# A fused transformer pair on one core: the first expert pair's rows summed from h, other weight slots, larger last pieces

## The chip, the cores and the metric

The program runs on one core of one Trainium2 chip. The metric is device time in microseconds (us) of one execution; smaller is better. The core has five engines with a queue each: PE (TensorE: matrix products and transposes), DVE (VectorE), ACT (ScalarE), POOL (GpSimd) and SP (SyncE, which here only starts transfers). Each engine takes its own instructions in the order in which they were laid down; semaphores tie the engines together. Transfers run on 16 DMA engines.

## What is computed

Two layers over 512 tokens of width 1024 in fp32. The first has a state-space and attention mixer and then a mixture of 64 experts; the second has a neighbourhood attention and a gated linear attention and then a dense feed-forward. The change lies in the experts:

```python
g_sel = argmax(t @ w_router_group)             # one of 8 groups for each token
top_logit, top_local = top_k(in_group, 2)      # two of its 8 experts
gate = softmax(top_logit) * p_group
# the tokens are sorted by expert into blocks; for each block:
hid = silu(xb @ w_gate[e]) * (xb @ w_up[e])    # 1024 -> 512
y_buf = hid @ w_down[e]                        # 512 -> 1024
y = zeros_like(t).at[tok_sorted].add(y_buf * gate)
```

Every expert has 6 MB of weights (gate, up and down, 2 MB each), and all 64 are read once.

## The kernel before, in words

**Experts in pairs.** Each expert gets 64 slots for tokens (more go through a loop that is entered only when one has more), so two experts fill the 128 rows of a product. `experts` (L973) walks over 32 pairs, i = 0 to 31. For a pair it multiplies the 128 gathered token rows (`xg`, turned so that the width lies on the partitions) by the gate and the up weights, 32 instructions for each (16 products with 64 output rows, in two instructions each), makes `hid`, turns it, multiplies by the down weights (32 instructions more), splits the result into a high and a low part and adds it back to the tokens of h with a 0/1 matrix (`combine`, L1162).

**The router.** The last output product of the mixer (`wout_tail`, L385) gives h in four tiles c of 128 tokens. As each is added up (L405), `route_tile` (L793) turns it, multiplies it by the router weights (L807) and writes the rows to `hd` in DRAM. `choose` (L863) finds the two experts and, by a product with a triangle of ones (L909, L910), the place of each token among its expert's; the result is `keys`. `gather_first` (L944) makes of the keys a 0/1 matrix `S0` for the first 256 slots (four experts, two pairs).

**The rows of a pair.** From pair 2 on the rows are fetched from `hd` by an indirect DMA on POOL's queue (`fetch`, L850) into one of four `rows` tiles, and turned by `gained` (L1021): eight PE transposes, and two DVE instructions that multiply by the norm's gain. For the first two pairs there is no fetch: `route_tile` splits h into a high part `hnH` (ACT, L812) and a low part `hnL` (POOL, L813), and `gather_first` multiplies both by `S0`, 16 matmuls of 256 columns for each token tile c, 64 in all, straight into the turned form; eight DVE instructions at L1042 bring it to `xg`.

**The weight slots.** Weights go through eight slots of 2 MB, used in turn (`ring`, L113), in the order G, U, D (gate, up, down) of each pair, two tiles each. Slots 0 to 2 lie in `ringp`, 3 and 4 in `ring2`, 5 in `ring3`, and 6 and 7 are the tiles tagged A1 and A2 (`w16x` in the profile). A1 and A2 hold the mixer's normed input first, and then `hnH` and `hnL`. So pair 0 fills slots 0 to 5, and the gate weights of pair 1 go to A1 and A2. All weights are started by SP in program order, so a tile that waits for its slot holds back all behind it. At most eight of SP's transfers are under way at a time; a tile goes in two pieces of 1 MB (four in the first six pairs, eight for pair 1's gate weights, L987).

**The last pair.** `pair` (L134) loads pair 31 in smaller pieces, the two experts' in turn, five for each tile. Behind it SP starts the second layer's first weights (L1729). The second layer's first transposes (`begin.turn`) lie among this pair's products.

**Order.** Instructions of an engine are laid down by a planner that may move them where nothing depends on it; the products of the expert loop are pinned to program order (L1000).

Of the kernel before, what the change touches and what calls it, by code (L numbers as in the profile page):

```python
# [6 lines left out]
FT = mybir.dt.float32  # L7
FR = mybir.dt.float32r
# [3 lines left out]
OP = mybir.AluOpType  # L12
# [3 lines left out]
P = 128  # L16
T = 512
D = 1024
KT = 8
NT = 4  # L20
# [8 lines left out]
class Net:  # L29
# [83 lines left out]
    def ring(self, shape, dma, parts=1):  # L113

        self.nring = getattr(self, "nring", -1) + 1
        n = [p.bufs for p in self.rings]
        m = self.nslots = sum(n) + (0 if self.held is None else 2)
        k = self.nring % m
        t = (self.held or {}).get(k)
        if t is None:  # L120
            if k >= sum(n):
                t = self.per.tile([P, 4096], FT, name="w16x", tag=("A1", "A2")[k - sum(n)])
            else:
                x = k
                for p, b in zip(self.rings, n):
                    if x < b:
                        break
                    x -= b
                t = p.tile([P, 4096], FT, name="w16", tag="w16")
            if self.held is not None:  # L130
                self.held[k] = t
        return self.load(t, shape, dma, parts)

    def pair(self, shape, dmas):  # L134

        tiles = [self.ring(shape, d, 0) for d in dmas]
        n, m = shape[1:]
        quarter = n // 4
        cuts = [(j, j + quarter, 0, m) for j in range(0, n - quarter, quarter)]
        cuts += [(n - 2, n - 1, 0, m), (n - 1, n, 0, m)] if n == 8 else [(n - 1, n, 0, m // 2), (n - 1, n, m // 2, m)]  # L140
        for a, b, c, d in cuts:
            for t, w in zip(tiles, dmas):
                self.nc.sync.dma_start(t[:, a:b, c:d], w[:, a:b, c:d])
        return tiles

    def load(self, t, shape, dma, parts=1):
# [610 lines left out]

    def route_start(self, keep, pool):
        nc, per = self.nc, self.per
        self.hn = (per.tile([P, NT, D], FR, name="hnH", tag="A1"), per.tile([P, NT, D], FR, name="hnL", tag="A2"))  # L760
        self.rpool = pool

        it = self.it = keep.tile([P, 512], FT, name="it")
        nc.gpsimd.iota(it.rearrange("p (e s) -> p e s", e=8), pattern=[[512, 8], [1, 64]], base=0,
                       channel_multiplier=0, allow_small_or_imprecise_dtypes=True)
        sk = self.sk = keep.tile([P, 32], FT, name="sk")
        for s in range(2):
            nc.gpsimd.iota(sk[64 * s:64 * s + 64, :], pattern=[[1024, 32]], base=512 * s, channel_multiplier=1,
                           allow_small_or_imprecise_dtypes=True)
        w64 = self.w64 = pool.tile([P, 64], FT, name="w64", bufs=1)  # L770
        nc.gpsimd.iota(w64, pattern=[[-1, 64]], base=64, channel_multiplier=0, allow_small_or_imprecise_dtypes=True)

# [12 lines left out]
        self.parts10 = keep.tile([P, NT, 5, 2], FR, name="parts10")  # L785

        self.hd = self.dram.tile([T, D], FT, name="hd")
        self.tops = keep.tile([P, 3, NT], FT, name="tops")
        self.S0 = keep.tile([P, NT, 256], FR, name="S0")
        self.keys = keep.tile([P, 2, NT], FT, name="keys")  # L790
        self.pl = self.psum("y")

    def route_tile(self, c):  # L793

        nc, V, h, pool, hn = self.nc, self.nc.vector, self.H, self.rpool, self.hn
        pl = self.pl[:, c * 72:(c + 1) * 72]
        xTs, turned = [], []
        for q in range(2):
            xT = pool.tile([P, 4, P], FT, name="xT", bufs=4)
            p = self.psum("sc")  # L800
# [8 lines left out]
                    self.order(t, m)  # L809
        V.tensor_copy(self.lg[:, c, :], pl)  # L810
        nc.scalar.dma_start(self.hd[c * P:(c + 1) * P, :], h[:, c, :])
        nc.scalar.copy(hn[0][:, c, :], h[:, c, :])  # L812
        nc.gpsimd.tensor_tensor(hn[1][:, c, :], h[:, c, :], hn[0][:, c, :].bitcast(FT), OP.subtract)  # L813
        sq = pool.tile([P, D], BF, name="sq", tag="xT", bufs=4)
        nc.scalar.activation(sq, h[:, c, :], AF.Square, accum_out=self.ss4[:, c:c + 1])

# [122 lines left out]
        self.nc.scalar.copy(self.counts, p[:, :64])  # L939

    def gather_start(self):
        self.first = [self.psum(t) for t in ("pj", "pj", "tp", "tp")]

    def gather_first(self, c):  # L944

        nc, V = self.nc, self.nc.vector
# [1 line left out]
        V.tensor_scalar(eq, self.it[:, :256], self.keys[:, 0, c:c + 1], None, op0=OP.is_equal)  # L948
        V.scalar_tensor_tensor(self.S0[:, c, :], self.it[:, :256], self.keys[:, 1, c:c + 1], eq, op0=OP.is_equal,
                               op1=OP.add)  # L950
        for j in range(KT):
            for part in range(2):
                nc.tensor.matmul(self.first[j // 2][:, (j % 2) * 256:(j % 2 + 1) * 256], self.hn[part][:, c, j::8],
                                 self.S0[:, c, :], start=c + part + j % 2 == 0, stop=j % 2 == 1 and c == 3 and part == 1)

    def route(self, keep, tail):

# [15 lines left out]
    def experts(self, keep, pool, front, inner, then):  # L973
        nc, i = self.nc, self.ins
# [15 lines left out]
        ahead = None  # L990

        self.rows = [front.tile([P, D], FT, name=f"rows{n}", bufs=1) for n in range(4)]
        for r in self.rows:
            nc.gpsimd.memset(r, 0.0)


# [16 lines left out]
        def values(q):  # L1013

            rs, gs, tok, at = self.slots(front, self.S0, [sk[:, 2 * q + x:2 * q + x + 1] for x in range(2)], 2)
            if q:
                for x in range(2):
                    self.fetch(self.rows[2 * (q % 2) + x], tok[:, x:x + 1])
            vals[q] = rs, gs, at

# [13 lines left out]
            yield  # L1034


        Xs, vals = {}, {}
        for x in range(2):
            Xs[x] = front.tile([P, KT, P], FT, name="xg", bufs=2)
        for x in range(2):  # L1040
            for n in range(4):
                V.tensor_tensor(Xs[x][:, 2 * n:2 * n + 2, :],  # L1042
                                self.first[n].rearrange("p (j s) -> p j s", j=2)[:, :, x * P:x * P + P],
                                self.g8[:, 2 * n:2 * n + 2].unsqueeze(2).to_broadcast([P, 2, P]), OP.mult)
        self.factors(front)
        self.gate(front)
        self.warm(AF.Silu, self.vals[:, 0, 2:3])
# [5 lines left out]
            for _ in range(min(n, len(todo))):  # L1053
                self.combine(*todo.pop(0), pin=True)

        evict = []
        for i in range(32):
            q, pr = i // 2, i % 2
            e0 = 2 * i
# [39 lines left out]
            next(turn, None)  # L1099
            bring(4)  # L1100
            next(turn, None)
            for e in evict:
                e()
            evict.clear()
            if pr == 0 and 0 < q < 15:
                values(q + 1)

# [2 lines left out]
            if not last:  # L1110
# [8 lines left out]
                    todo.extend((ST, yH, yL, t, hs) for t in range(NT))  # L1119
                if i == 0:  # L1120
                    values(1)
            else:
                ys = [self.psum(t) for t in ("y", "pj")]
                for j in range(4):
# [679 lines left out]
```

## Time and profile before

| | |
|---|---|
| runs | 2073.59, 2072.85, 2068.12 us; median 2072.85 us |
| profiled execution | 2071.55 us, of it the span of the core 2069.8 us |
| busy PE, DVE, ACT, POOL | 1954.0 (94%), 962.6 (47%), 537.4 (26%), 204.6 (10%) us |
| HBM read | 500.15 MB, 245 GB/s over the span; 415 to 426 GB/s from about 466 to 1294 us |
| chain that ended last | DMA 46%, PE 43%, DVE 6% |

A row of a timeline is: start, length in us, engine, line, operation, out<-in, shapes, count; in square brackets the idle time of the engine before it and what ended that. PE's busy time is modelled and counts overlapping matmuls once. The granted clock of PE is given as a share of full speed: 1.00 is 2.4 GHz, 0.50 is 1.2 GHz.

### The profile page before, as it was taken

The numbers are of one execution on the slowest core, as the hardware profiler recorded it, in microseconds if no ns is written. First come the engines' busy times: TensorE is split into PE (matmuls) and PEld (weight loads), VectorE is DVE, ScalarE is ACT, GpSimd is POOL, SyncE is SP. The second block draws the span as 40 slices with busy tenths as digits, with TensorE's granted clock in tenths as the row PEclk, the third lists the DMA queues.
The fourth block names the chain that finished last, engine by engine and source line by source line (L and its number), as shares of the span: only waits on it lengthen the run. The fifth ranks groups of instructions, "written<-read, shape, count | busy, mean of one in ns | idle before, by whom it ended". The sixth has DMA issues, their size and how long they took to land.

```text
span 2069.8 us, 24164 instructions
## 1 busy us (share of the span) xinstructions
PE 1954.0 (94%) x9551; PEld 1227.6 (59%) x9551; DVE 962.6 (47%) x1899; ACT 537.4 (26%) x902; POOL 204.6 (10%) x252
## 2 busy tenths in 40 slices
PE   7999999999999999999999999998999999999998
PEld 6788777744443344344334334346777778888886
DVE  5774667743532343243243333334564664344345
ACT  5773545311000100000010000024352423232232
POOL 5111324210000000000000000002111100000000
PEclk9999999999999999999999999999999899999999
DMA  7312112579999999999999999983212112223221
GB/s 201 111 42 82 58 66 82 201 290 416 415 424 424 423 425 425 424 423 426 424 424 423 422 423 424 393 314 67 90 41 82 42 41 92 83 81 122 84 80 41
DMA packets 116939, 494.04 MB, mean 239 GB/s; under 512 B 16658, under 2 KB 23257, under 8 KB 78424
## 3 DMA queue, kind: packets, MB, share of 16 engines
q1 hardware_dynamic: 110024, 483.64, 58.5%
q0 software_dynamic: 6208, 6.74, 1.5%
q10 hardware_dynamic: 592, 2.10, 0.3%
q8 instruction: 76, 1.25, 0.2%
q14 instruction: 39, 0.32, 0.0%
HBM read 500.15 MB, written 6.15 MB: 245 GB/s over the span
## 4 chain that ended last, share of the span: by engine, by line
DMA 46%; PE 43%; DVE 6%; ACT 2%; issue 2%; SPq 1%; POOL 0%; DVEq 0%; ACTq 0%; POOLq 0%
DMA w<-in_w_up 8%; DMA w<-in_w_down 8%; PE pj L185 7%; PE pj L184 7%; DMA w<-in_w_gate 7%; PE pj L186 7%; DMA w16x<-in_w_up 7%; DMA w16x<-in_w_gate 7%; DMA w16x<-in_w_down 7%; PE sc L185 3%; PE sc L184 3%; PE sc L186 3%; DMA w<-in_w_in 1%; DVE M L703 1%; PE y L185 1%
## 5 line engine op out<-in xcount | busy, mean ns | idle before, releaser
L1001 PE MATMUL pj<-w,xg 128*64 128x512 f32 x1536 | 370.0, 609 | 36.1 <-DMA w<-in_w_up 35.0
L1001 PEld LDWEIGHTS pj<-w,xg 128*64 128x64 f32 x1536 | 121.2, 140 | 273.9 <-issue 213.4
L165 DVE TENSOR_TENSOR wL<-w,wH 128x1024 fp32r<-128x1024 f32 x135 | 168.4, 1248 | 203.5 <-ACT wH L164 202.7
L1088 DVE SCALAR_TENSOR_TENSOR hid<-pj,slots,hid 128x512 f32<-128x512 f32 x32 | 24.0, 751 | 464.3 <-PE pj L1001 464.3
L164 ACT CAST wH<-w 128x1024 fp32r<-128x1024 f32 x136 | 142.3, 1048 | 340.3 <-PE pj L185 166.9
L1169 DVE TENSOR_TENSOR H<-sc,H 128x512 f32<-128x512 f32 x256 | 161.5, 682 | 9.5 <-PE sc L1166 7.1
L1001 PE MATMUL pj<-w16x,xg 128*64 128x512 f32 x512 | 126.1, 615 | 17.1 <-DMA w16x<-in_w_up 15.0
L1166 PE MATMUL sc<-yH,ST 128*128 128x512 f32 x256 | 113.2, 442 | 0.6 <-DVE H L1169 0.6
L1097 ACT COPY hT<-tp 128x512 f32<-128x512 f32 x32 | 18.8, 587 | 352.1 <-PE tp L1095 352.1
L852 POOL DMA_INDIRECT rows<-hd,tok x30 | 30.3, 1009 | 806.5 <-issue 646.7
L186 PE MATMUL pj<-n3H,wL 128*128 128x512 f32 (+1 forms) x272 | 103.6, 381 | 0.8 <-DVE wL L165 0.8
L184 PE MATMUL pj<-n3H,wH 128*128 128x512 f32 (+1 forms) x272 | 103.6, 381 | 0.0
L185 PE MATMUL pj<-n3L,wH 128*128 128x512 f32 (+1 forms) x272 | 103.5, 381 | 0.0
L184 PE MATMUL pj<-A,wH 128*128 128x512 f32 x240 | 97.8, 408 | 4.0 <-ACT wH L164 2.8
L1166 PE MATMUL sc<-yL,ST 128*128 128x512 f32 x256 | 101.1, 395 | 0.0
L185 PE MATMUL sc<-wL,mixH 128*128 128x512 f32 x252 | 98.5, 391 | 0.0
L184 PE MATMUL sc<-wH,mixH 128*128 128x512 f32 x252 | 98.5, 391 | 0.0
L186 PE MATMUL sc<-wH,mixL 128*128 128x512 f32 x252 | 98.2, 390 | 0.0
L1001 PEld LDWEIGHTS pj<-w16x,xg 128*64 128x64 f32 x512 | 39.6, 141 | 98.7 <-issue 72.4
L185 PE MATMUL pj<-A,wH 128*128 128x512 f32 x240 | 97.7, 407 | 0.0
L186 PE MATMUL pj<-A,wL 128*128 128x512 f32 x240 | 96.9, 404 | 0.5 <-DVE wL L165 0.5
L1001 PE MATMUL y<-w,hT 128*64 128x512 f32 x384 | 89.4, 608 | 0.7 <-ACT hT L1097 0.7
(579 smaller groups left out, 3382.5 us busy)
## 6 DMA issues: line engine op xcount, KB each, us to landing
w<-in_w_gate SPq DMA_DIRECT2D x76, 1024.0 KB, 19.6
w<-in_w_down SPq DMA_DIRECT2D x76, 1024.0 KB, 19.6
w<-in_w_up SPq DMA_DIRECT2D x72, 1024.0 KB, 20.9
w<-in_w_ff SPq DMA_DIRECT2D x16, 2048.0 KB, 7.9
w16x<-in_w_up SPq DMA_DIRECT2D x28, 1024.0 KB, 19.7
w<-in_w_in SPq DMA_DIRECT2D x12, 2048.0 KB, 10.9
w16x<-in_w_down SPq DMA_DIRECT2D x24, 1024.0 KB, 20.5
w16x<-in_w_gate SPq DMA_DIRECT2D x24, 1024.0 KB, 20.4
```

What stands on the lines that cost most here:

```text
L164: a = nc.scalar.copy(H, src)
L165: b = (engine or nc.vector).tensor_tensor(L, src, H.bitcast(FT), OP.subtract)
L184: m = mm(out, lH, rH, start=first, stop=False)
L185: mm(out, lH, rL, start=False, stop=False)
L186: mm(out, lL, rH, start=False, stop=last)
L703: nc.vector.tensor_tensor(t, t, cb[g], OP.mult)
L852: self.nc.gpsimd.indirect_dma_start(out=rows, out_offset=None, in_=self.hd[:, :], in_offset=bass.IndirectOffsetOnAxis(ap=tok, axis=0), bou ...
L1001: return self.pin(nc.tensor.matmul(*a, **k))
L1088: V.scalar_tensor_tensor(hid, pu, r, hid, op0=OP.mult, op1=OP.mult)
L1097: nc.scalar.copy(hT.rearrange("p j s -> p (j s)"), p)
L1166: m = nc.tensor.matmul(p, ST[:n, t * P:(t + 1) * P], y[:n], start=k == 0, stop=k == 1)
L1169: nc.vector.tensor_tensor(h[:, t, hs], p, h[:, t, hs], OP.add)
```

## The change

Four things change.

- `hnH` and `hnL` and the instructions that make them are gone. `gather_first` makes `S0` as before, and then sums only the 128 slots of pair 0, in plain order: for each token tile two fp32 products of 512 columns with `S0` as the stationary side and h itself as the moving side, into two banks of PSUM. Behind the router one bank is copied to `rows[0]` by DVE and the other by ACT, and `gained(0)` turns them as for any later pair.
- Pair 1's rows are fetched like all later ones: `values(0)` starts one fetch, and `gained(1)` stands behind the down products of pair 0, with its two DVE instructions right behind.
- The slots' order is: `ringp`, `ringp`, `ring2`, `ring2`, A1, A2, `ringp`, `ring3`. A1 and A2 hold pair 0's down weights; pair 1's gate weights go to the third slot of `ringp` and to `ring3`.
- The last pair is loaded in two pieces for a gate or up tile, and three for a down tile (a half and two quarters).

```diff
@@ ring
-            if k >= sum(n):
-                t = self.per.tile([P, 4096], FT, name="w16x", tag=("A1", "A2")[k - sum(n)])
+            p = self.rings[0 if self.held is None else (0, 0, 1, 1, 0, 0, 0, 2)[k]]
+            if self.held is not None and k in (4, 5):
+                t = self.per.tile([P, 4096], FT, name="w16x", tag=("A1", "A2")[k - 4])
             else:
...
@@ pair
-        cuts = [(j, j + quarter, 0, m) for j in range(0, n - quarter, quarter)]
-        cuts += [(n - 2, n - 1, 0, m), (n - 1, n, 0, m)] if n == 8 else [(n - 1, n, 0, m // 2), (n - 1, n, m // 2, m)]
-        for a, b, c, d in cuts:
+        for a, b in [(0, n // 2), (n // 2, n)] if n == 8 else [(0, 2), (2, 3), (3, 4)]:
...
@@ route_tile
-        nc.scalar.copy(hn[0][:, c, :], h[:, c, :])
-        nc.gpsimd.tensor_tensor(hn[1][:, c, :], h[:, c, :], hn[0][:, c, :].bitcast(FT), OP.subtract)
@@ gather_start, gather_first
-        self.first = [self.psum(t) for t in ("pj", "pj", "tp", "tp")]
+        self.first = [self.psum("tp") for _ in range(2)]
...
-        for j in range(KT):
-            for part in range(2):
-                nc.tensor.matmul(self.first[j // 2][:, (j % 2) * 256:(j % 2 + 1) * 256], self.hn[part][:, c, j::8],
-                                 self.S0[:, c, :], ...)
+        for half in range(2):
+            nc.tensor.matmul(self.first[half], self.S0.bitcast(FT)[:, c, :P], self.H[:, c, 512 * half:512 * half + 512],
+                             start=c == 0, stop=c == 3)
@@ experts
-        for r in self.rows:
+        for r in self.rows[1:]:
             nc.gpsimd.memset(r, 0.0)
...
-            if q:
-                for x in range(2):
+            for x in range(2):
+                if q + x:
                     self.fetch(self.rows[2 * (q % 2) + x], tok[:, x:x + 1])
...
-        for x in range(2):
-            for n in range(4):
-                V.tensor_tensor(Xs[x][:, 2 * n:2 * n + 2, :], ...)
+        for half in range(2):
+            (nc.scalar.copy if half else V.tensor_copy)(self.rows[0][:, 512 * half:512 * half + 512], self.first[half])
+        for _ in gained(0):
+            evicted()
...
                 if i == 0:
                     values(1)
+                    for _ in gained(1):
+                        evicted()
```

## Rows read from the trace of the kernel before

**Rows 1.** Chain of waits, 1300 to 1420: start us, us, what.
```profile
1310.63 19.78 DMA w16x<-in_w_up
...
1330.46 7.08 PE pj L1001 x30
```

**Rows 2.** Timeline of SP's queue, 290 to 520.
```profile
341.61 5.59 SPq L155 DMA_DIRECT2D w<-in_w_gate  x8
...
406.11 2.14 SPq L155 DMA_DIRECT2D w<-in_w_down  x4
426.52 9.37 SPq L155 DMA_DIRECT2D w16x<-in_w_gate  x16
436.79 5.38 SPq L155 DMA_DIRECT2D w<-in_w_up  x8
```

**Rows 3.** Waits of SP's queue, 400 to 430: us in total, times, longest.
```profile
SPq L155 <- DVE H L405: 23.1, 1, 23.1
SPq L155 <- PE tp L953: 18.2, 1, 18.2
```

**Rows 4.** Windows: stretch, length, busy by engine, PE clock, DMA share, GB/s.
```profile
341.60:355.00 13.40, 12.45 (x70) 9.52 (x68) 7.98 (x11) 8.06 (x11) 4.71 (x5) 1.00 0.86 314
...
426.50:450.00 23.50, 21.88 (x93) 7.76 (x94) 8.45 (x33) 3.10 (x6) 0.44 (x2) 0.88 0.96 355
```

**Rows 5.** Timeline of PE, 426 to 470: the gate and up products of two pairs.
```profile
426.62 8.01 PE L1001 MATMUL pj<-w,xg 128*64 128x512 f32 x32
...
435.55 7.09 PE L1001 MATMUL pj<-w,xg 128*64 128x512 f32 x32
...
454.71 7.09 PE L1001 MATMUL pj<-w16x,xg 128*64 128x512 f32 x32
```

**Rows 6.** Groups by line, DVE, 380 to 427: busy us, mean ns.
```profile
L901 DVE SCALAR_TENSOR_TENSOR t<-M,t 128x64 f32<-128x64 bf16 x4 | 5.1, 1286 | 0.0
```

**Rows 7.** Timeline of all engines, 392 to 422: the router's end.
```profile
395.62 2.37 POOL L813 TENSOR_TENSOR hnL<-H,hnH 128x1024 fp32r<-128x1024 f32 x1 [3.02 <-ACT hnH L812]
...
400.09 1.11 PE L807 MATMUL y<-wr,xT 128*128 128x72 f32 x8 [1.73 <-DVE xT L803]
...
406.24 0.23 DVE L901 SCALAR_TENSOR_TENSOR t<-M,t 128x64 f32<-128x64 bf16 x1
...
410.33 0.23 DVE L810 COPY lg<-y 128x72 f32<-128x72 f32 x1 [1.71 <-PE y L807]
...
416.90 0.28 DVE L915 CUSTOM_DVE_ANT_0 e<-sc,M,first 128x64 f32<-128x64 f32 x1 [1.67 <-PE sc L910]
...
417.24 3.02 DVE L948 TENSOR_SCALAR eq<-it,keys 128x256 f32<-128x256 f32 x1
...
417.38 3.76 POOL L994 MEMSET rows<- 128x1024 f32 x4
...
421.81 0.48 DVE L949 SCALAR_TENSOR_TENSOR S<-it,keys,eq 128x256 fp32r<-128x256 f32 x1
```

**Rows 8.** Windows of the router's end: PE's granted clock is third from the right.
```profile
402.00:403.00 1.00, 1.00 (x4) 0.76 (x3) 0.93 (x6) 0.00 (x0) 0.00 (x0) 0.50 0.00 0
...
422.00:424.00 2.00, 1.56 (x6) 1.59 (x7) 1.22 (x7) 1.49 (x2) 0.12 (x1) 0.50 0.00 0
```

**Rows 9.** Timeline: a plain fp32 product, four transposes of rows, their eviction.
```profile
368.38 0.83 PE L714 MATMUL sc<-BC,st 128*128 128x128 f32 x6
...
469.64 0.60 PE L1028 MATMUL pj<-ident,rows 128*128 128x128 f32 x4
...
470.67 0.68 DVE L1030 TENSOR_TENSOR xg<-pj,g 128x512 f32<-128x512 f32 x1
```

**Rows 10.** The `rows` tiles: the fetches' time to landing.
```profile
DMA to landing us min/median/max: 6.9/8.4/10.6
```

**Rows 11.** Windows of the last pair: DMA share, GB/s at the end.
```profile
1340.00:1350.00 10.00, 10.00 (x49) 4.46 (x49) 5.22 (x9) 0.96 (x2) 0.00 (x0) 1.00 0.82 291
```

**Rows 12.** Waits of PE's weight loads, 1345 to 1392.
```profile
PEld pj L1001 <- DMA w<-in_w_up: 0.9, 3, 0.4
```

More of the change, by code (lines that the diff above doesn't have):

```diff
@@ L120, in ring @@
         if t is None:
-            if k >= sum(n):
-                t = self.per.tile([P, 4096], FT, name="w16x", tag=("A1", "A2")[k - sum(n)])
-            else:
[L124 to L128, printed above, removed]
+            p = self.rings[0 if self.held is None else (0, 0, 1, 1, 0, 0, 0, 2)[k]]
+            if self.held is not None and k in (4, 5):
+                t = self.per.tile([P, 4096], FT, name="w16x", tag=("A1", "A2")[k - 4])
+            else:
                 t = p.tile([P, 4096], FT, name="w16", tag="w16")
@@ L137, in pair @@
         n, m = shape[1:]
-        quarter = n // 4
-        cuts = [(j, j + quarter, 0, m) for j in range(0, n - quarter, quarter)]
-        cuts += [(n - 2, n - 1, 0, m), (n - 1, n, 0, m)] if n == 8 else [(n - 1, n, 0, m // 2), (n - 1, n, m // 2, m)]
-        for a, b, c, d in cuts:
+        for a, b in [(0, n // 2), (n // 2, n)] if n == 8 else [(0, 2), (2, 3), (3, 4)]:
             for t, w in zip(tiles, dmas):
-                self.nc.sync.dma_start(t[:, a:b, c:d], w[:, a:b, c:d])
+                self.nc.sync.dma_start(t[:, a:b], w[:, a:b])
         return tiles
@@ L759, in route_start @@
         nc, per = self.nc, self.per
-        self.hn = (per.tile([P, NT, D], FR, name="hnH", tag="A1"), per.tile([P, NT, D], FR, name="hnL", tag="A2"))
         self.rpool = pool
@@ L793, in route_tile @@
     def route_tile(self, c):
-        nc, V, h, pool, hn = self.nc, self.nc.vector, self.H, self.rpool, self.hn
+        nc, V, h, pool = self.nc, self.nc.vector, self.H, self.rpool
         pl = self.pl[:, c * 72:(c + 1) * 72]
@@ L950, in gather_first @@
                                op1=OP.add)
-        for j in range(KT):
-            for part in range(2):
-                nc.tensor.matmul(self.first[j // 2][:, (j % 2) * 256:(j % 2 + 1) * 256], self.hn[part][:, c, j::8],
-                                 self.S0[:, c, :], start=c + part + j % 2 == 0, stop=j % 2 == 1 and c == 3 and part == 1)
+        for half in range(2):
+            nc.tensor.matmul(self.first[half], self.S0.bitcast(FT)[:, c, :P], self.H[:, c, 512 * half:512 * half + 512],
+                             start=c == 0, stop=c == 3)
     def route(self, keep, tail):
@@ L1034, in gained, with evicted @@
             yield
-        Xs, vals = {}, {}
-        for x in range(2):
-            Xs[x] = front.tile([P, KT, P], FT, name="xg", bufs=2)
-        for x in range(2):
-            for n in range(4):
-                V.tensor_tensor(Xs[x][:, 2 * n:2 * n + 2, :],
-                                self.first[n].rearrange("p (j s) -> p j s", j=2)[:, :, x * P:x * P + P],
-                                self.g8[:, 2 * n:2 * n + 2].unsqueeze(2).to_broadcast([P, 2, P]), OP.mult)
+        Xs, vals, evict = {}, {}, []
+        for half in range(2):
+            (nc.scalar.copy if half else V.tensor_copy)(self.rows[0][:, 512 * half:512 * half + 512], self.first[half])
+        def evicted():
+            for e in evict:
+                e()
+            evict.clear()
+        for _ in gained(0):
+            evicted()
         self.factors(front)
@@ L1054, in bring @@
                 self.combine(*todo.pop(0), pin=True)
-        evict = []
         for i in range(32):
@@ L1101, in experts @@
             next(turn, None)
-            for e in evict:
-                e()
-            evict.clear()
+            evicted()
             if pr == 0 and 0 < q < 15:
@@ L1121, in experts @@
                     values(1)
+                    for _ in gained(1):
+                        evicted()
             else:
```

## The prediction

> **What bounds the kernel now.** I read the page first: PE is busy for 94% of the span, yet the chain that ended last gives 46% to DMA, and from 466 to 1294 us the transfers run at 415 to 426 GB/s without a gap. So I asked for the chain of waits in order of time. From 429 us to 1330 us it is one transfer of weights after the other; the last of them is the up weights of pair 30, which land at 1310.63 + 19.78 = 1330.41 us, and PE starts on them 0.05 us later [rows 1]. Behind that the chain is PE's. So the expert stage lasts as long as a stream of fixed size takes from its start, and what matters is when that stream starts for good.
>
> SP's timeline shows the start [rows 2]. Pair 0's six tiles come early (341.61 the gates, 406.11 the last down tile). Then SP stands for 18.2 us, until PE has read `hnH` and `hnL` for the last time [rows 3]; at 426.52 it starts pair 1's gate weights into A1 and A2, and at 436.79 its up weights. A window from 426.5 to 450.0 moves 355 GB/s x 23.5 us = 8.34 MB [rows 4], which is those four tiles (8.39 MB). So the stream's first mark is: pair 1's up weights are in at 450.0 us. The same event that frees A1 and A2, the end of the gather, also lets PE start pair 0, at 426.62 [rows 5]. I call this T; the mark lies at T + 23.4.
>
> **The change, part by part.**
>
> *Slots.* A1 and A2 lose their reader L953, so pair 0's down weights go there as soon as SP comes to them, behind the tiles it starts before 379 us. Pair 1's first gate tile gets a slot of `ringp`, which is free by then, and its second `ring3`, which was free at 406.11 [rows 2, 3]. All eight tiles are then in before PE starts pair 0. The DMA engines fall idle, and the next tile, pair 1's up, waits for slot 0, that is for the end of pair 0's gate products: 8.0 us after T' (the new start) as now [rows 5], or 8.9 with a longer stretch at the low clock; I take 8.5. From rest, two tiles started at 341.61 took until about 354.1 (314 GB/s x 13.4 us = 4.2 MB, [rows 2, 4]), 12.5 us; with 0.2 for SP the mark is at T' + 21.2. If T' were equal to T this alone gives 23.4 - 21.2 = 2.2 us, since 10 us of gate transfers are taken out of the stream but the stream can't start before slot 0 is free. Every microsecond by which T' is earlier comes on top.
>
> *The stalls of DVE.* L901 takes 0.23 us when it runs alone, but its four take 5.1 us, because two of them stand beside POOL's L813, 2.37 us [rows 6, 7]. Without L813 that is 5.1 - 4 x 0.23 = 4.2 us less on DVE. On the path: PE waits 1.73 us at 398.4 to 400.1, and then runs at a granted 0.50 around 402 [rows 7, 8], which I read as some 3.5 us of work stretched by 1.7. Ahead of the last logits also stand ten of the first 16 gather matmuls, of which two fp32 products remain. Nothing if PE was the limit anyway, 6 if all of it is on the path; I take 5, the row nearest to it being L901's. ACT's four copies to `hnH` cost nothing on the path and save nothing.
>
> *From the last logits to S0.* These are now at 410.33 and 421.81 + 0.48 = 422.29, 12.0 us apart. In it DVE waits 1.67 us for a place product that stands in PE's queue behind gather matmuls, and L948 takes 3.02 us beside four memsets of 3.76 us [rows 7]. Three memsets remain, so 0.9 of this goes for sure, with the 1.67 and some 0.7 (an estimate, less than half of a stall by [rows 6]) for the last L813, beside which DVE works too, 3.3. If the memsets come to lie elsewhere it is 6, if only one memset's share counts 0.9. I take 3.3.
>
> *From S0 to the first product.* Now 426.62 - 422.29 = 4.3 us, 16 matmuls. After: two fp32 products of 512 columns. The trace has none with 128 output rows. An expert product shares the array with another, 32 instructions in 7.09 us [rows 5], which makes 0.22 x 2 x 2 = 0.89 us for a whole one; L714, three products of 128 columns in 0.83 us [rows 9], gives 0.28 x 4 = 1.1. So 1.8 to 2.2 for two, at full clock. Then a copy of about 0.68, four transposes 0.60, an eviction 0.68 [rows 9], and some 0.6 for four hand-overs: 4.4 us. But PE has less to do in the router's end than now, and even now it is granted 0.50 from 422 to 424 after a wait [rows 8]. At half clock products and transposes double, 6.8 us. A stop in ACT's queue ahead of its copy would add some 1.3, an estimate below the stops of 1.67 and 1.73 us in [rows 7]. So 0 to +3.8; I take +2.2.
>
> The Trainium skill ("TensorE: Matmul & The Clock Gate", "What's actually happening") says that "the default state is throttled, and activity releases the throttle", which speaks against taking matmuls out of this stretch. By that rule the step is the whole 6.8 us and the first products of pair 0 are slow too; the row of 422 to 424 agrees as far as it goes.
>
> Together T' = 426.62 - 5.0 - 3.3 + 2.2 = 420.5, and the mark is at 441.7 instead of 450.0: 8.3 us.
>
> *Pair 1's rows.* `values(0)` follows the gate products; the fetch is on POOL's queue at about T' + 10.7 and lands 6.9 to 10.6 us later [rows 10], at T' + 21 at the latest. It is used behind pair 0's down products, at T' + 28, as pair 1 starts now at 454.71 = T + 28.1 [rows 5]. POOL has nothing else queued behind it. The eight transposes add 1.2 us to PE and some 0.6 for the eviction, so pair 1 starts at T' + 30. That is hidden: its up weights are in at T' + 21, and the slots stay ahead. The tightest turn: pair 2's gates take pair 0's down slots, free at T' + 28, and the stream comes to them at T' + 21.2 + 10.1 = T' + 31. Without that cover it costs up to 2 us.
>
> *The last pair.* 30 transfers become 14. Now the DMA engines fall to 291 GB/s there [rows 11]. But PE's weight loads wait only 0.9 us for these weights [rows 12], so I take 0.9 of gain, from 0 to 2. Coarser halves cost nothing so long as they land first; after 1330 us the stream needs 16.8 MB / 0.42 = 40 us, each tile before PE comes to it.
>
> The Trainium skill ("DMA: Bandwidth & Descriptors", "Measured") advises batches of at least 1 MiB for 75% of peak. The slower pieces agree. Were the stream the limit to the end, the 12.6 MB would take 30 instead of some 36 us and the sum would be 6 larger; the row of the waits speaks against it.
>
> **The sum.** 8.3 + 0.9 = 9.2 us off the profiled execution's 2071.55 us (span 2069.8 and 1.75 around it): 2062.4. The median of the runs is 1.3 above that execution and the lowest 3.4 below it.
>
> **Rivals.**
> 1. *The route's end hardly gets shorter.* PE is cold through the new hand-over and the memsets stay in the way. For: the 0.50 of [rows 8], and three of four memsets remain. Against: the stalls beside L813 go in any order. With 2 for the stalls, 0.9 for the memset and +3.8 for the hand-over T' = 427.5, the mark is 1.3 us earlier: 2069.4 with the last pair's 0.9; up to 2066 this is no change.
> 2. *All of it counts.* 6, 6 and 0 give T' = 414.6: 14.2 us, and 2 at the end: 2055.4. For: the waits are on one chain. Against: PE's own work in 380 to 410 leaves little to gain.
> 3. *The in-order queues turn against it.* Slower: `rows[0]` is now copied by DVE and ACT, and if these copies are laid behind the router's factors (square root, exponentials, their tables), the sum waits for that chain, and the ring stands empty meanwhile, since all eight slots are full and none is free until pair 0's gates are used. It decides from T' = 450.0 - 21.2 = 428.8. With nothing gained on the stalls but 2, and 6 to 10 us of hand-over more, T' = 426.6 - 2 + 12 = 436.6, the mark 7.8 later: 2078.5. For: now L242's chain lies in that same place. Against: nothing makes the planner wait there, and these copies are ready first.
> 4. *A1 and A2 are not what holds the stream.* Then only the stalls count, and the order of slots gives nothing: 2071.55 - 6.1 - 0.9 = 2064.6, inside the range.
>
> **How the numbers follow.** The forecast with rival 4 has 0.62, rival 1 0.20, rival 2 0.11, rival 3 0.07. A measurement here tells some 0.3% from no change, 6.2 us. The forecast's own range is 2058 to 2066.5 us, a little of which lies within 0.3%. So faster 0.70, same 0.22, slower 0.08. For eight in ten I reach from 2055.5 to 2069.5.
>
> **What would show it.** After: L813, L812 gone and every L901 near 0.25 us. SP starts `w16x<-in_w_down` before 385 us and pair 1's gates before 410; the DMA engines stand still between about 413 and T' + 8.5. The first L1001 starts near 420 us (415 to 428), and pair 1's up weights land 21 us later. The chain is again all DMA to the up weights of pair 30, which land near 1322, and the second layer keeps its length. I am wrong in the mechanism if the first L1001 starts early but the stream doesn't keep that lead, by gaps in the transfers before 600 us; or if PE waits for pair 1's rows; and in the last term if PE waits longer for the larger pieces.

## The result, and the profile after

The changed kernel takes 2058.16 us in the median (2057.0 to 2063.64, 5 runs), the kernel before 2072.85 us (2068.12 to 2074.01, 5 runs). The ratio of the means is 0.9942, 95% interval [0.9927, 0.9957]: faster by 12.0 us (8.9 to 15.1); the medians lie 14.7 us apart. The profiled span went from 2069.8 to 2055.2 us, 14.6 us less; I forecast 9.2.

The chain of waits of the changed kernel (start us, us, what):

```profile
413.56 3.79 PE tp L943 x4
419.51 7.09 PE pj L991 x32
427.59 7.07 PE pj L991 x32
436.15 11.64 DMA w<-in_w_down
...
1296.84 19.70 DMA w<-in_w_up
1316.58 7.08 PE pj L991 x30
```

L943, L991 and L892 are here what L953, L1001 and L901 were. Pair 0's products start at 419.51, not 426.62 us [rows 5]. From 436.15 on the chain is one transfer after the other again, until pair 30's up weights land at 1296.84 + 19.70 = 1316.54 us. Before, that was 1330.41 [rows 1]: 13.9 us earlier.

The last piece of pair 1's up weights is started at 428.00 in the changed kernel and at 441.84 before. From start to landing they take, first in the changed kernel, then before:

```profile
DMA to landing us min/median/max: 9.4/9.4/9.4
```

```profile
DMA to landing us min/median/max: 9.8/9.8/9.8
```

So pair 1's up weights are in at 437.4 us instead of 451.6, 14.2 us earlier, and the 879 us behind that hand on the lead nearly unchanged.

SP's queue of the changed kernel, 355 to 450:

```profile
360.69 3.89 SPq L149 DMA_DIRECT2D w16x<-in_w_down  x8
...
376.69 5.59 SPq L149 DMA_DIRECT2D w<-in_w_up  x8
383.40 22.35 SPq L149 DMA_DIRECT2D w<-in_w_gate  x15
421.48 6.90 SPq L149 DMA_DIRECT2D w<-in_w_up  x8
```

Pair 0's down weights start at 360.69, ahead of its up weights at 376.69 (the planner has moved them), and fifteen of the sixteen pieces of pair 1's gates at 383.40 to 405.75; before, those gates came from 426.52 on, into A1 and A2 [rows 2]. The next start is pair 1's up weights, at 421.48: 2.0 us behind the first product, where I had put 8.5. Two windows of the changed kernel around it (stretch, length, busy by engine, PE's granted clock, DMA share, GB/s), and the one of 413 to 418 for the clock:

```profile
413.00:418.00 5.00, 3.78 (x4) 1.17 (x4) 2.73 (x13) 0.81 (x3) 0.35 (x1) 0.52 0.00 0
413.00:424.00 11.00, 9.42 (x34) 3.78 (x36) 4.63 (x19) 3.88 (x7) 0.79 (x3) 0.78 0.13 28
424.00:440.00 16.00, 14.38 (x72) 5.37 (x69) 5.49 (x19) 1.27 (x2) 1.22 (x1) 1.00 0.99 364
```

The DMA engines stand nearly still before 424 (28 GB/s), and are full after it. The end of the router, in the changed kernel's timeline:

```profile
404.83 0.23 DVE L803 COPY lg<-y 128x72 f32<-128x72 f32 x1 [1.44 <-PE y L800]
...
409.22 3.02 DVE L939 TENSOR_SCALAR eq<-it,keys 128x256 f32<-128x256 f32 x1
...
409.37 2.73 POOL L984 MEMSET rows<- 128x1024 f32 x3
...
413.02 0.48 DVE L940 SCALAR_TENSOR_TENSOR S<-it,keys,eq 128x256 fp32r<-128x256 f32 x1
...
413.56 3.78 PE L943 MATMUL tp<-H,S 128*128 128x512 f32 x4 [0.85 <-DVE S L940]
```

The last logits are at 404.83 instead of 410.33, S0 is ready at 413.50 instead of 422.29 [rows 7]. DVE's compare L939 still takes 3.02 us beside the memsets, and the last sums take 3.78 us at a clock of about 0.52 (1.2 GHz), where the four of the token tile before took 1.96 us. The mask's product, by groups of lines (busy us, mean ns), has lost its stalls [rows 6]:

```profile
L892 DVE SCALAR_TENSOR_TENSOR t<-M,t 128x64 f32<-128x64 bf16 x4 | 0.9, 226 | 0.0
```

### The profile page after: what moved, and what is told of

Read it like the earlier page. It is cut to its first block, busy times and chain, and to the rows that moved or that the text cites. A ratio compares the mean times of both kernels' runs of the same rounds, so it can differ in the third digit from the quotient of the medians.

```text
span 2055.2 us, 24059 instructions
## 1 busy us (share of the span) xinstructions
PE 1943.0 (95%) x9519; PEld 1228.8 (60%) x9519; DVE 955.6 (46%) x1896; ACT 533.8 (26%) x899; POOL 196.3 (10%) x248
## 4 chain that ended last, share of the span: by engine, by line
PE 46%; DMA 44%; DVE 5%; ACT 3%; issue 1%; POOL 0%; SPq 0%; DVEq 0%; ACTq 0%; POOLq 0%
DMA w<-in_w_down 14%; DMA w<-in_w_up 14%; DMA w<-in_w_gate 13%; PE pj L179 7%; PE pj L178 7%; PE pj L180 7%; PE sc L179 3%; PE sc L178 3%; PE sc L180 3%; PE pj L991 2%; DMA w<-in_w_in 1%; DVE M L697 1%; PE y L180 1%; PE y L178 1%; PE y L179 1%
## 5 line engine op out<-in xcount | busy, mean ns | idle before, releaser
L991 PE MATMUL pj<-w,xg 128*64 128x512 f32 x1536 | 369.1, 612 | 39.4 <-DMA w<-in_w_up 36.4
L991 PEld LDWEIGHTS pj<-w,xg 128*64 128x64 f32 x1536 | 126.8, 141 | 270.8 <-issue 202.1
L991 PE MATMUL pj<-w16x,xg 128*64 128x512 f32 x512 | 125.1, 602 | 10.5 <-DMA w16x<-in_w_up 10.5
L991 PEld LDWEIGHTS pj<-w16x,xg 128*64 128x64 f32 x512 | 47.8, 138 | 82.2 <-issue 60.1
L991 PE MATMUL y<-w,hT 128*64 128x512 f32 x384 | 91.8, 599 | 0.7 <-ACT hT L1088 0.7
```

Of the source, the lines that this page charges most:

```text
L991: return self.pin(nc.tensor.matmul(*a, **k))
```

## The experiments

All times below are of profiled executions; the ratios are to the kernel before, run beside them. "First logits" is the eviction of the first token tile's logits: runs reach that point up to 3.8 us apart (382.5 to 386.3), and two profiles of the same router code (before and e6) are 1.05 us apart there, so steps behind it are best compared as differences from it.

| kernel | first logits | last logits | first product | pair 1's up started | pair 30's up landed | ratio |
|---|---|---|---|---|---|---|
| before | 384.92 | 410.33 | 426.62 | 436.79 | 1330.41 | 1 |
| after | 384.55 | 404.83 | 419.51 | 421.48 | 1316.54 | 0.9942 [0.9927, 0.9957] |
| e1 | 382.49 | 402.80 | 414.68 | 416.64 | 1312.13 | 0.9926 [0.9912, 0.9941] |
| e2 | 384.49 | 404.79 | 419.88 | 428.27 | 1322.20 | 0.9955 [0.9942, 0.9969] |
| e3 | 382.60 | 402.90 | 417.58 | 419.55 | 1313.71 | 0.9947 [0.9932, 0.9962] |
| e4 | 382.52 | 402.82 | 417.91 | 420.71 | 1316.63 | 0.9942 [0.9928, 0.9956] |
| e5 | 384.19 | 404.49 | 419.57 | 422.93 | 1319.23 | 0.9932 [0.9921, 0.9944] |
| e6 | 385.97 | 409.82 | 426.19 | 437.10 | 1330.75 | 1.0004 [0.9995, 1.0014] |
| e7 | 385.76 | 406.05 | 421.14 | 434.92 | 1329.94 | 0.9986 [0.9977, 0.9994] |
| e8 | 385.89 | 406.19 | 416.39 | 418.35 | 1315.65 | 0.9916 [0.9903, 0.9929] |
| e9 | 386.14 | 407.60 | 422.45 | 424.41 | 1319.74 | 0.9952 [0.9935, 0.9968] |
| e10 | 386.10 | 406.38 | 422.30 | 425.09 | 1321.18 | 0.9938 [0.9923, 0.9953] |
| e11 | 384.50 | 407.71 | 422.81 | 426.10 | 1321.50 | 0.9961 [0.9946, 0.9976] |
| e12 | 386.28 | 406.56 | 416.76 | 418.72 | 1314.24 | 0.9937 [0.9922, 0.9953] |

One column gives the next: in all fourteen, pair 30's up weights land 893.6 to 897.3 us after pair 1's up weights are started, though that start lies anywhere from 416.6 to 437.1 us. From that landing to the end of the span it is 737.4 to 742.7 us, and of the ratios only those of e6 and e7 have an interval that does not overlap the changed kernel's. So it is the columns that carry the argument, and the ratios only bear them out.

**When the stream starts again: e2.** Pair 1's up tiles as one transfer of 2 MB each instead of four of 512 KB:

```diff
-                    [self.ring([P, KT, 512], wu[e0 + s], n) for s in range(2)],
+                    [self.ring([P, KT, 512], wu[e0 + s], 1 if e0 == 2 else n) for s in range(2)],
```

> The kernel after, with pair 1's up weights started as one transfer of 2 MB each instead of four of 512 KB, so that they wait until the whole gate tile of pair 0 has been read. Theory A (the stream restarts 2 us behind the first product because each piece waits only for its own part of the slot): the restart comes 5 us later, and so does the landing of pair 30's up weights; ratio about 0.9965. Theory B: pair 1's up weights are not needed for 25 us, so nothing changes, ratio 0.994.

SP's queue and the end of the chain in this run:

```profile
428.27 0.80 SPq L149 DMA_DIRECT2D w<-in_w_up  x2
```

```profile
1302.48 19.72 DMA w<-in_w_up
1322.24 8.78 PE pj L991 x30
```

The start goes from T' + 2.0 to T' + 8.4 (T' is the first product), right behind the end of pair 0's gate products (419.88 + 8.36 = 428.24), and the landing comes 5.7 us later. The ratio shows some 2.7 us of that, inside its interval. So in the changed kernel each piece waits only for the products that read its own part of slot 0: the first is free as soon as PE is past it. In e4, e5, e10 and e11 the start is at T' + 2.8 to 3.4, and the first 32 products take 7.9 to 8.5 us there instead of 7.09, behind stretches with a granted clock of 0.50.

**What was loaded before the start: e7.** The two tiles of pair 1's gate weights held until GpSimd's last splitting instruction behind the places:

```diff
+        for k, p in ((6, self.rings[0]), (7, self.rings[2])):
+            t = self.held[k] = p.tile([P, 4096], FT, name="w16", tag="w16")
+            self.order(done, nc.gpsimd.memset(t...[:, :, :1], 0.0))
```

> The changed kernel, but the two tiles for pair 1's gate weights are held by GpSimd until its last splitting instruction behind the places, so that their load starts about where it did before the change and not at 383 us. Theory (the loads form one bound stream from the first expert product on, and what is already in the tiles then is work that the stream doesn't have to do): the two tiles' ten us come back into the stream, the landing of pair 30's up weights moves from 1316.5 to between 1322 and 1328 us with the first product where it is in the changed kernel, ratio 0.997 to 1.000. Rival (only the start of the expert products counts): the landing moves by less than 2 us, ratio 0.994 to 0.995.

SP's queue and the end of the chain:

```profile
389.96 43.19 SPq L149 DMA_DIRECT2D w<-in_w_gate  x24
434.92 5.48 SPq L149 DMA_DIRECT2D w<-in_w_up  x8
```

```profile
1310.23 19.71 DMA w<-in_w_up
1329.99 8.78 PE pj L991 x30
```

The 24 starts are pair 0's eight, which this edit also moves, from 341 us to between 389.96 and 407.70, and pair 1's sixteen, which a window from 420 to 434 shows by themselves:

```profile
423.47 9.69 SPq L149 DMA_DIRECT2D w<-in_w_gate  x16
```

The DMA engines stand still from 413 to 423.4 us (0 GB/s), so pair 0's weights are in before PE starts on them. The first product comes as early, counted from the first logits, as in the changed kernel (35.4 and 35.0 us), yet the landing is back at 1329.94, and 0.9986 is most of the way back. The rival, by which only PE's start counts, is out. The cost, 13.4 us (12.2 counted from the first logits), is more than the 5.5 to 11.5 expected: the held gates start at T' + 2.3 and stand ahead of pair 1's up weights in SP's queue, which start at T' + 13.8 instead of T' + 2.0.

**The order of the slots by itself: e3.** The old order (the rings first, A1 and A2 last) without the hold of `hnH` and `hnL`:

```diff
-            p = self.rings[0 if self.held is None else (0, 0, 1, 1, 0, 0, 0, 2)[k]]
-            if self.held is not None and k in (4, 5):
+            p = self.rings[0 if self.held is None else (0, 0, 0, 1, 1, 2, 0, 0)[k]]
+            if self.held is not None and k in (6, 7):
```

> The kernel after, with the slots in the order of before (pair 0's tiles in the first six, pair 1's gates in A1 and A2), but A1 and A2 free early since the split of h is gone. Theory A: all eight tiles are in before the first product in this order too, so the restart and the end move by less than 1 us; ratio 0.994. Rival (the order of slots is itself worth something, by which tile waits for which): up to 5 us later, ratio 0.9965.

Pair 1's gates are then loaded into A1 and A2 from 358.68 on, the up weights start again at T' + 2.0, and the ratio can't be told from the changed kernel's. With e7, what counts is that A1 and A2 have no reader in the gather any more, not which tile goes where.

**The memsets: e1 and e10.** In e1 the `rows` tiles are set to zero behind GpSimd's last splitting instruction; in e10 it is done where it was, in eight pieces of 128 columns each:

```diff
@@ e1
-        for r in self.rows[1:]:
-            nc.gpsimd.memset(r, 0.0)
...
+        for r in self.rows[1:]:
+            self.order(done, nc.gpsimd.memset(r, 0.0))
@@ e10
-            nc.gpsimd.memset(r, 0.0)
+            for j in range(8):
+                nc.gpsimd.memset(r[:, j * P:j * P + P], 0.0)
```

> The kernel after, with the three memsets of the rows tiles laid behind the router's factors on POOL, so that they no longer stand beside DVE's key instructions (the 0/1 compare took 3.02 us there against 0.35 us elsewhere). Theory A (the stage lasts from the first expert product on, one for one): the first expert product comes 2.7 us earlier, 4.5 if the shorter wait also keeps TensorE at full clock, the up weights of pair 30 land as much earlier, and the ratio to the kernel before falls from 0.9942 to 0.992 or 0.993. Theory B (what counts is that eight weight tiles are in early, the exact start doesn't matter): no change of the landing of pair 30, ratio 0.994.

> The changed kernel with the three expert tiles' memsets (0.91 us each, 1024 columns) written as eight of 128 columns each, at the same place. Theory (the same rule: VectorE waits for the end of one instruction of GpSimd, not for all of them): the compare of the last token tile takes 0.35 to 0.7 us instead of 3.02, the first expert product comes about 2.5 us earlier after it (10.3 us from compare to product in the changed kernel, 7.5 with the memsets behind the router), ratio about 0.9928. Rival (VectorE is kept out as long as GpSimd has memsets in a row): the compare takes 2.5 us or more, ratio 0.994.

Compare and last sums in e1:

```profile
407.18 0.36 DVE L939 TENSOR_SCALAR eq<-it,keys 128x256 f32<-128x256 f32 x1
...
408.84 3.67 PE L943 MATMUL tp<-H,S 128*128 128x512 f32 x4 [0.88 <-DVE S L940]
```

Compare and memsets in e10:

```profile
410.75 3.86 DVE L939 TENSOR_SCALAR eq<-it,keys 128x256 f32<-128x256 f32 x1
...
410.90 3.57 POOL L985 MEMSET rows<- 128x128 f32 x24
```

With the memsets out of the way the compare takes 0.36 us, and from compare to first product it is 7.5 us instead of 10.3. Counted from the first logits, the first product comes 2.8 us earlier than in the changed kernel, as expected, and the landing 2.4. Cutting the memsets up doesn't help: the compare waits through all 24 pieces, 0.15 us each, so its wait is not for one instruction of GpSimd. My theory of e10 fell.

The code before has four memsets, and its two profiles differ. Compare and next instruction, in the kernel before and in e6:

```profile
420.18 1.02 DVE L899 TENSOR_SCALAR M<-w,v 128x64 bf16<-128x64 f32 x1
```

```profile
416.73 3.92 DVE L945 TENSOR_SCALAR eq<-it,keys 128x256 f32<-128x256 f32 x1
420.57 0.23 DVE L896 TENSOR_SCALAR M<-w,v 128x64 bf16<-128x64 f32 x1
```

In the kernel before, the compare is through at 420.26, behind three of the four memsets [rows 7], and the instruction behind it takes 1.02 us beside the fourth, which ends at 421.14. In e6 the compare waits through all four. In the changed kernel that instruction takes its 0.23 us:

```profile
412.16 0.23 DVE L890 TENSOR_SCALAR M<-w,v 128x64 bf16<-128x64 f32 x1
```

So the fourth memset did cost 0.8 to 0.9 us, in one place or the other.

**The clock in the hand-over: e8.** As e1, and six unread transposes behind each of the last token tile's two place products:

```diff
+            if c == NT - 1:
+                self.busy(mt, 6)    # six transposes of h into a bank of PSUM that nobody reads
```

> The changed kernel with the expert tiles' memsets behind the router (as in the run with the late memsets), and six transposes that nobody reads behind each of TensorE's two place products of the last token tile, so that TensorE is not idle while VectorE makes the last tile's selection. Theory (TensorE's clock is at its lower level there because it had little to do, and that is what makes the last four sums take 3.7 us instead of 1.9): the sums take about 1.9 us, the first expert product comes 1.8 to 2.5 us earlier than with the late memsets alone (7.5 us after the compare there), ratio about 0.9917. Rival (the clock doesn't follow, or the transposes hold up the sums): the first product stays or is up to 1 us later, ratio 0.9925 to 0.993.

The last sums in e8, and a window of the clock (columns as above):

```profile
412.23 1.99 PE L952 MATMUL tp<-H,S 128*128 128x512 f32 x4 [0.19 <-DVE S L949]
```

```profile
412.00:417.00 5.00, 3.80 (x18) 1.97 (x18) 3.98 (x16) 3.11 (x7) 0.59 (x1) 1.00 0.00 0
```

The granted clock is 1.00 in 412 to 417 (before the sums PE was busy for 3.62 us of 4), where it was 0.52 in the changed kernel (0.26 of 4 busy ahead of that) and 0.55 in e1's sums, 408.8 to 412.6. The sums take 1.99 us, and the first product is 5.8 us behind the compare. The place products of e8 come no later. Of the 1.7 us by which the first product is earlier than in e1, counted from the first logits, nothing is left at the landing in this profile (929.8 us in e8, 929.6 in e1, 932.0 in the changed kernel). The Trainium skill ("TensorE: Matmul & The Clock Gate", "What's actually happening") has it that activity releases the throttle; by that rule unread work pays here, and the traces of e1 and e8 agree.

**GpSimd beside the router: e5, e9, e11.** The subtraction that the change took out is put back with a result that nobody reads: e5 as eight of 128 columns per token tile, e9 as one of 1024 columns (1.89 us, where the one taken out had 2.37) behind ScalarE's squares, e11 the same one ahead of them. The edit of e11:

```diff
+        nc.gpsimd.tensor_tensor(sq, h[:, c, :], h[:, c, :], OP.subtract)
         nc.scalar.activation(sq, h[:, c, :], AF.Square, accum_out=self.ss4[:, c:c + 1])
```

> The changed kernel with GpSimd's eight subtractions of 128 columns per token tile put back beside the router (into a tile that nobody reads); 32 subtractions that write nothing of use, all else as in the changed kernel. Theory (the shorter route sets the end): the router's VectorE instructions wait for GpSimd again as they did before the change, the last logits come about 5 us later than in the changed kernel (404.8 us there, 410.3 before), the first expert product and the landing of pair 30's up weights come later by as much, and about five of the twelve us won are gone: ratio to the kernel before about 0.9965. Rival (the subtractions lay beside other work and the gain comes from elsewhere, the earlier loads above all): first product within 1 us, ratio 0.994.

> The changed kernel with one GpSimd subtraction over all 1024 columns per token tile beside the router, of the length that the one taken out had (2.36 us); its result lies in a tile that nobody reads. The run with eight subtractions of 128 columns (0.41 us each) in its place left the last logits where they were (404.5 us against 404.8). Theory (a VectorE instruction that meets one on GpSimd waits until that one ends, so the length of the single instruction counts): the mask's product on VectorE takes 1.5 us or more in some token tiles instead of 0.23 to 0.34, the last logits come 2 to 5 us later than in the changed kernel, the landing of pair 30's up weights as much later (1316.5 there), ratio 0.995 to 0.9965. Rival (VectorE gave way, but TensorE was the limit there anyway, and the 5.5 us come from the gather products that left its queue): last logits within 1 us of 404.8, ratio 0.994.

> As the run with one GpSimd subtraction over 1024 columns per token tile (1.89 us there), but placed ahead of ScalarE's squares instead of behind them, so that it starts where the token tile is complete. In that run two of its four met VectorE's compares, which the next logits don't wait for, and one met the mask's product, which they do; first to last logits took 21.5 us, against 20.3 in the changed kernel and some 25.4 before the change, where two met the mask's product and TensorE then ran at its lower clock. Theory (the 5 us are those stalls, TensorE's waits behind them and the clock that falls in these waits): with two or more of the four in the way of what the logits wait for, first to last logits takes 23 to 25.5 us, and the ratio is 0.995 to 0.9965. Rival (a stall costs what it takes and the clock stays): 21 to 22.5 us, ratio 0.9945 to 0.995.

In e5's timeline, the mask's product beside the short pieces:

```profile
387.18 1.84 POOL L808 TENSOR_TENSOR spare<-H 128x128 f32<-128x128 f32 x4
...
388.23 0.39 DVE L896 SCALAR_TENSOR_TENSOR t<-M,t 128x64 f32<-128x64 bf16 x1
```

In e9's, with the held compare:

```profile
389.72 1.89 POOL L807 TENSOR_TENSOR sq<-H 128x1024 bf16<-128x1024 f32 x1 [3.58 <-ACT sq L806]
...
389.78 1.91 DVE L893 SCALAR_TENSOR_TENSOR t<-M,t 128x64 f32<-128x64 bf16 x1
...
399.52 1.65 DVE L940 TENSOR_SCALAR eq<-it,keys 128x256 f32<-128x256 f32 x1
```

In e11's, with the two held maskings and the last logits:

```profile
385.03 1.43 DVE L876 SCALAR_TENSOR_TENSOR e<-lg,tops,w 128x8 f32<-128x8 f32 x1
...
393.85 1.69 DVE L876 SCALAR_TENSOR_TENSOR e<-t,tops,w 128x64 f32<-128x64 f32 x1
...
403.11 1.90 POOL L806 TENSOR_TENSOR sq<-H 128x1024 bf16<-128x1024 f32 x1 [4.34 <-issue]
403.17 1.91 DVE L893 SCALAR_TENSOR_TENSOR t<-M,t 128x64 f32<-128x64 bf16 x1
...
407.71 0.23 DVE L803 COPY lg<-y 128x72 f32<-128x72 f32 x1 [0.98 <-PE y L800]
```

First to last logits take 20.3 us in the changed kernel and in e5, 21.5 in e9, 23.2 in e11, and 25.4 before. e5 met its rival's expectation and not its theory's, but it was a poor copy: its pieces of 0.41 us let DVE in between, nothing moves, and so it says nothing against the theory. In e9 one mask's product is held for 1.91 us and the others of GpSimd's four meet work that the logits don't wait for (a compare of 1.65 us), in e11 one mask's product (1.91) and two maskings of logits (1.43 and 1.69): of 1.7 us more on the way in e9 1.2 come out, of 4.3 us in e11 2.9. e9's 1.2 lie between what its theory (2 to 5) and its rival (less than 1) expected; e11's 23.2 is at the lower end of its theory's 23 to 25.5, but the clock fall that this theory counted in did not come: the granted clock is 1.00 from 384 to 408 us. The landing comes 5.0 us later in e11, counted from the first logits: 2.9 from the logits, 0.4 from there to the first product, 1.3 from the later restart (T' + 3.3), and 0.3 within the stream. The ratios, 0.9952 and 0.9961, fit, but overlap with the changed kernel's. The Trainium skill ("SBUF — State Buffer", "Who interferes with whom") says that the later one of a DVE instruction with two inputs in SBUF and a GpSimd instruction that reads SBUF is blocked for the whole of the other; e9 and e11 agree. For DVE's faster two-port form, which by that page an instruction of the compare's kind can take, it says the same, one instruction long; e10 shows a wait through a run of 24, and the kernel before one through three of four.

**The last pair: e4 and e6.** e4 is the changed kernel with the old small pieces, e6 the kernel before with the large ones:

```diff
-        for a, b, c, d in cuts:
+        for a, b in [(0, n // 2), (n // 2, n)] if n == 8 else [(0, 2), (2, 3), (3, 4)]:
```

> The kernel after, with the last pair loaded in the small pieces of before. In the changed kernel TensorE took 42.3 us from the landing of pair 30's up weights to the last up product, before 41.4 us. Theory A (the tail is TensorE's): within 1 us, perhaps 0.9 us better, ratio 0.9935 to 0.995; the transfers at the end are slower (below 350 GB/s in the ten microseconds after pair 30) without effect. Rival (the larger pieces are worth 6 us of transfer time): 6 us slower, ratio 0.997.

> The kernel before with one part of the change alone: the last pair's weights in larger pieces. Theory (by the run with the small pieces in the changed kernel: the tail behind the last pair's up weights is TensorE's own time): ratio 1.000, within 0.0007, pair 30's up weights land where they did before (1330.5 us), and the last up products end 42 to 43.5 us after that. Rival (the larger pieces keep the queue fuller and the loads behind the last pair come sooner): 3 to 6 us off, ratio 0.997 to 0.9985.

The large pieces do keep the DMA engines fuller, as two rows of windows show, first the changed kernel's, then e4's:

```profile
1320.00:1330.00 10.00, 10.00 (x50) 5.64 (x48) 6.14 (x10) 0.59 (x1) 0.00 (x0) 1.00 1.01 425
```

```profile
1320.00:1330.00 10.00, 10.00 (x48) 5.56 (x46) 6.05 (x10) 0.59 (x1) 0.00 (x0) 1.00 0.85 308
```

PE is busy for the whole 10 us in both. From the landing to the transposes of the last pair's products it is 42.4 us before and in e4, 43.2 after: 0.8 worse, not better. All fourteen profiles agree once those are compared in which pair 30's 30 up products take as long. With 7.08 us for these, the last up products end 41.4 us behind the landing with the small pieces (before, e4) and 42.3 with the large (the changed kernel, e8 to e11); with 8.65 to 8.78 us, 43.1 with the small (e12) and 43.9 to 44.0 with the large (e1, e2, e3, e5, e6, e7). Alone, the edit gives 1.0004. Nothing is left of the 6 us that the stream might have gained.

e6 also shows the unchanged router a second time. The same two mask's products are held (2.27 and 2.43 us), but the clock stays up, where it was 0.50 in [rows 8]:

```profile
402.00:403.00 1.00, 1.00 (x10) 0.86 (x9) 0.71 (x5) 0.00 (x0) 0.07 (x1) 1.00 0.00 0
```

First to last logits take 23.9 us there, not 25.4. So 1.6 us of the profiled gain is a fall of the clock that the old code shows in one of two profiled executions.

**The two better edits together: e12.** e8 with e4's small pieces:

> The two edits that the earlier runs found better than the changed kernel's, together: memsets behind the router with the unread transposes (0.9916 by itself), and the last pair's weights in the old small pieces (0.6 to 0.8 us less from the landing of pair 30's up weights to the last up products). Theory: they add up, ratio 0.991 to 0.9916. Rival (the smaller pieces are worth nothing in the whole time, as their run by itself showed 0.9942 like the changed kernel): 0.9916 to 0.9925.

The first product is 30.5 us after the first logits, as in e8 and 4.5 us sooner than in the changed kernel, but the ratio is 0.9937, above e8's and outside both expectations, so both missed. The two intervals overlap from 0.9922 to 0.9929, and the size of the pieces can't make that difference (e4, e6). In the two profiles the difference lies behind the landing: e12's pair 30 lands 1.4 us before e8's, but from there to the end it is 742.7 us, the longest of the fourteen, and 738.5 in e8; 3.3 us of that lie behind the last pair's down products, where no edit reaches. So e8's ratio may have been lucky and e12's unlucky. That moving the memsets and keeping TensorE busy pays is shown for the first product, and for the whole time it is not settled.

## Why the prediction was right, and where its sizes were off

The mechanism held: the end follows the one start of the stream, and the two things that move that start are an earlier T' and the gates that are in already. The number held with some luck. The median, 2058.16, is 0.2 us inside the range of 2058 to 2066.5; the profiled execution, to which the sum was added up, is outside it with 2057.0. One term was 4.9 us short and the last pair's 1.7 us too good, and the profiled gain holds 1.6 us of a clock fall that not every execution has.

- *The stream sets the end.* Right up to the landing, which comes 893.6 to 897.3 us behind the start of pair 1's up weights in every kernel. Behind it come 737.4 to 742.7 us that vary by themselves.
- *Stalls up to the last logits, -5.0.* Measured -5.1 from the first logits (25.4 to 20.3). The stalls are shown (e9, e11): 2.9 us came back in e11, and of the 5.1 us 1.6 belong to the clock's fall (e6), which I had counted in as part of every execution. The ten gather matmuls that stood ahead of the logits were not tried by themselves.
- *From the logits to S0, -3.3.* 12.0 became 8.67 us: right, and in its parts too. The wait of 1.67 us is gone; a masking beside the last L813, 0.96 us before, takes 0.23; and the 0.9 for the fourth memset came not in the compare, which takes 3.02 us in both, but in the instruction behind it (1.02 us, now 0.23).
- *Hand-over, +2.2.* It went from 4.33 to 6.01, +1.7, by the low clock as reasoned (e8: 4.2). The other reading, 6.8 us and slow first products, is met in part: pair 0's first products take 7.09 us in the changed kernel, but 7.9 to 8.5 in six of the twelve experiments. Together T' is 419.5, forecast 420.5.
- *The restart at T' + 8.5, and the mark at T' + 21.2.* This is the step that failed. I let pair 1's up weights wait for the end of pair 0's gate products; they start in pieces at T' + 2.0, and are in at 437.4, T' + 17.9. The mark before was also read too early: the last piece landed at 451.6, T + 25.0, not at 450.0. So these two marks are worth 7.1 us beside the change of T', where I had 2.2: 4.9 us too little, and most of what separates 8.3 from the 13.9 measured. e2 is my forecast made true: there the start is at T' + 8.4, and pair 30's up weights land at 1322.2, where I had put them (near 1322). Of the 15.3 us by which that start is earlier than before, 7.1 are PE's earlier start; the other 8.2 are there because it follows PE's start by 2.0 us and not by 10.2, the gates being in already (e7).
- *Pair 1's rows hidden.* Right. Its gate products start at 447.2, T' + 27.7, and PE waits for no fetch.
- *The last pair, -0.9.* Wrong in sign: +0.8 (e4), and nothing that shows in the whole time alone (e6).
- *Rival 4, A1 and A2 are not what holds the stream.* Refuted by e7; the order of slots alone is worth nothing that shows (e3). *Rival 2*, all of it counts, gave 2055.4, nearer than the forecast, but by other sizes: its T' was 414.6. Of *rival 1* both conditions occurred (the compare still takes 3.02 us, the clock is 0.52 in the sums), but at less than its prices: the hand-over cost 1.7 and not 3.8 us, and the stalls gave 5.1 and not 2. *Rival 3* didn't occur: T' lies 9.3 us ahead of its 428.8.

With the marks at T' + 17.9 and T + 25.0 my own T' gives 438.4 instead of 451.6, and nothing for the last pair: 13.2 us, between the 12.0 of the runs and the 14.6 of the one pair of profiles.

## What to carry to other kernels

Where a stream of transfers bounds a stage, ask two things of a change in front of it: which instruction lets the first piece go (piece by piece, not tile by tile), and what is already loaded by then; here both came out one for one, within 4 us, where the stream ended. What stands before the stream counts only through that one start, so a wait of 2 us there is worth as much as 2 us anywhere on the way to it. Price a stall from a place where the same two instructions met, and look at a second execution before a fall of the clock goes into the sum.

## What the runs showed that was not expected

- A compare of DVE (128 x 256, 0.35 us) takes 3.02 us beside three memsets of GpSimd and 3.86 us beside the same memsets in 24 pieces, though a memset only writes. Beside four it got through behind the third in one execution (3.02 us) and behind the fourth in another (3.92 us). Whether a gap between them would let it in was not tried.
- Twelve unread transposes of 128 columns took the last four sums from 3.7 to 2.0 us.
- The up products of pair 30 take 7.08 us in some executions and 8.78 in others, of kernels that differ only far ahead of them. The wait before them is much the same, but behind it the granted clock is 1.00 in the changed kernel (1316.5 to 1324 us) and 0.78 in e1 (1312.1 to 1320 us). With the 737.4 to 742.7 us from that landing to the end, a difference of 1 to 2 us between the spans of two single profiles is no evidence here.
